# SSD mixer in a hybrid decoder layer: both decay planes of a chunk in one double-buffered tile, one copy of their ends, and convolution tails read from PSUM

## The chip, the core and the metric

The kernel runs on one core of a Trainium2 chip. The metric is the device time of one execution in microseconds; a run's time is that of the whole launch, and the profile's span is from the first to the last instruction. The engines are TensorE (PE; its weight loads are PEld), VectorE (DVE), ScalarE (ACT), GpSimd (POOL), and SyncE (SP), which issues nearly all DMAs.

## The reference

One layer on 2048 tokens of width 1024, in float32. A normalised input goes through one large projection. Its columns feed a sparse attention (an indexer scores keys, the best 256 of each query are kept) and an SSD mixer; both results go through an output projection, and a dense MLP with a squared ReLU follows. Cut to the SSD part:

```python
xbc = conv(xbc)                                  # causal, width 4, depthwise
X = (xs * dt[..., None])                         # 16 chunks of 128 tokens, 8 heads
A_cs = jnp.cumsum(Adt, axis=-1)
Lmat = jnp.exp(segsum(Adt))                      # decays inside a chunk
cb = jnp.einsum("bclhn,bcshn->bhcls", Cc, Bc) * Lmat
y_diag = jnp.einsum("bhcls,bcshp->bclhp", cb, X)
decay_states = jnp.exp(A_cs[..., -1:] - A_cs)
states = jnp.einsum("bclhn,bhcl,bclhp->bchpn", Bc, decay_states, X)
...
y_off = jnp.einsum("bclhn,bchpn,bhcl->bclhp", Cc, states, jnp.exp(A_cs))
y = y_diag + y_off
```

The convolution needs the last three tokens of the tokens before it; these are the tails of the kernel.

## The kernel before, in words

Tokens are worked on in four tiles of 512. A front stage runs `in_proj(t)` for the four tiles. Every product of the large projections is split into high and low parts (`mm3`, L257, L260, L261), which read weights (wr, split by POOL and ACT into wh and wl) and a moving operand u. For each of eight column groups of the convolution (L364 to L374) `raw` receives three old columns from `tails` (L367), the scaled product from PSUM (L329), and then its last three columns are copied to `tails` (L369); three multiply-adds (L374) make `pre`. The results are written to DRAM (s_d).

`ssd(t)` runs 32 pieces in all: 4 tiles x 4 chunks x 2 head groups. A piece has an `enter`, a `carry`, and every second one a `leave`. `enter` loads si (L483) and the cumulative decays cb (L486, the same row in all partitions). VectorE adds a mask, lm = cb + trineg (L487). ScalarE takes four exponentials of lm (L489) and one of cb (L490). VectorE copies the last column of each plane to `ends` (L492, L493). TensorE transposes and multiplies into p_x (L496, L497); VectorE scales it to xd (L500), GpSimd multiplies with ends (L501), VectorE multiplies lm with p_x (L503), and GpSimd cb with si (L504), both in place. `carry` makes p_y from lm, xd, cb and the state st (L514, L515), p_st (L517), updates the state (L518, L519) and adds the skip (L521). `leave` normalises (L530 to L543) and stores to mix_d (L546). lm has one buffer, cb two, si three, xd one.

The back stage runs four windows, each an output projection `out_proj(t)` (p_acc, its eviction L793, the residual sum L802, transposes L807, operands u of the next products L810) and then `mlp(t)` (up products with r, L834, and down products p_dn). Top-k selection (`topk`, L611 to L643: 32 counting passes on ACT with L618 and L619 on DVE behind each, then seven passes L633 to L643 over the scores) and `attention` are woven into front and windows. A pacing function (`weave`) issues their steps at set points with a priority for each kind; a scheduler with a timeline of its own then places the instructions on each engine, so that a change of a wait or of a dependence moves rows elsewhere too. Each engine runs its rows strictly in that order.

Of the kernel before, what the change touches and what calls it, by code (L numbers as in the profile page):

```python
# [16 lines left out]
OP = mybir.AluOpType  # L17
# [4 lines left out]
P = 128  # L22
L = 2048
D = 1024
T = 512
# [16 lines left out]
def hybrid_layer(ctx, tc, x, x_t, w_cols, n_post_mix, n_post_mlp, w_in, w_misc, dt_bias, a_log, d_skip,  # L42
                 w_out, w_up, w_down, rel_bias, c_ident, c_flip, c_stack, c_tri, c_trineg, c_caus, c_bucket, out, dbg=None):
    nc = tc.nc
    V, S, G, PE, SP = nc.vector, nc.scalar, nc.gpsimd, nc.tensor, nc.sync
# [15 lines left out]
    ATT = dict(c2=2, qs=2)  # L61
    FRONT = dict(c4=FC, x24=1, m4=2, m2=3, kc=2, tq=1, mk=1)
    BACK = dict(c4=BC, x8=2, g4=9, m2=2)
    SSD = dict(si=3, cb=2, lm=1, xd=1)
    SIDE = [dict(kc=3, tq=1, mk=1), dict(kc=2, tq=1)]
    BANKS = [dict(tp=3, po=1), dict(tp=3, po=1)]
    where = {}
# [7 lines left out]
    def place(tag):  # L75

        if tag in rings:
            rings[tag].append(rings[tag].pop(0))
            return rings[tag][-1]
        return where[tag]  # L80

    def tl(tag, shape, dt=F32, name=None):
        pool, bufs, slot = place(tag)
        return pool.tile(shape, dt, tag=name if tag in ("s", "ks", "ssm") else slot, name=name or tag, bufs=bufs)

    def phase(name, sizes, smalls=None, side="left"):
        stack = ExitStack()
        pool = stack.enter_context(tc.tile_pool(name=name, bufs=1, side=side, reuse_waits="tile"))
        use(pool, sizes)
        if smalls:  # L90
            use(pool, {smalls: 2})
        return stack

    def once_tile(name, shape, dt=F32):
        return where["ssm"][0].tile(shape, dt, name=name, bufs=1)
# [6 lines left out]
    def pt(tag, name=None):  # L102
        pool, bufs, slot = place(tag)
        return pool.tile([P, 512], F32, tag=slot, name=name or tag, bufs=bufs)
# [15 lines left out]

    scan = phase("scan", SSD, "ssm", "right")
    front = phase("front", FRONT, "s")
# [67 lines left out]
    tails = once_tile("tails", [P, 8, 3])  # L190
# [74 lines left out]
    def proj(ap, u, w=None, how='00'):  # L265

        m = ap.shape[-1]
        w = w or load_w(ap, [P, KT, m], how)
        p = pt("mm", "p_mm")
        for k in range(KT):  # L270
            hi, lo = w[k // 4]
            mm3(p[0:m], hi[:, k % 4, :], lo[:, k % 4, :], u[k][:, 0, :], u[k][:, 1, :], k == 0, k == KT - 1)
        return p
# [13 lines left out]
    def row_spread(rs, tag="mm"):  # L287
        p = pt(tag, "p_rs")
        for b in range(NB):
            PE.matmul(p[:, b * P:(b + 1) * P], rs[:, b:b + 1].broadcast_to([P, P]), ident, start=True, stop=True)  # L290
        rsb = tl("rsb", [P, T])
        V.tensor_copy(rsb, p)
        return rsb
# [26 lines left out]
    def in_proj(t):  # L320
# [5 lines left out]
        else:  # L326
            rsb = row_spread(state["rs", t], TB)
# [4 lines left out]
        p = proj(w_misc, u, w, how=HI_)  # L332
        if t == 0:
            row_scale(0)
            rsb = row_spread(state["rs", 0], "acc")
# [5 lines left out]
        p = pt(TB, "p_tr")  # L341
# [22 lines left out]
        for m in range(8):  # L364
            p = proj(w_in[m], u, how=HI_)
            raw = tl("m2", [P, T + 4], name="raw")
            V.tensor_copy(raw[:, 0:3], tails[:, m, :])  # L367
            scaled(raw[:, 3:T + 3], p)
            V.tensor_copy(tails[:, m, :], raw[:, T:T + 3])  # L369
            acc = pre[:, m, :]  # L370
            tap_w = lambda j: cols[:, 16 + j * 8 + m:17 + j * 8 + m]
            S.activation(acc, raw[:, 3:T + 3], AF.Identity, scale=tap_w(3), bias=cols[:, 48 + m:49 + m])
            for j in range(3):
                V.scalar_tensor_tensor(acc, raw[:, j:T + j], tap_w(j), acc, op0=OP.mult, op1=OP.add)  # L374
            if m == 1:
                p = pt(TB, "p_tr")
                for b in range(NB):
                    PE.transpose(p[0:DH, b * P:(b + 1) * P], ki[:, b, :], ident)
                kf = tl("m2", [DH, T], name="kf")
                S.activation(kf, p[0:DH], AF.Identity, scale=cols[0:DH, 60:61], bias=cols[0:DH, 61:62])  # L380
                hs = KI[0:DH, t0:t0 + T]
                S.activation(hs, kf, AF.Copy)
                V.tensor_tensor(KI[DH:P, t0:t0 + T], kf, hs.bitcast(F32), op=OP.subtract)
            yield 5.2
# [13 lines left out]
        for m in range(4):  # L398
            p = proj(w_in[8 + m], u, how=HI_)
# [9 lines left out]
        p = proj(w_in[12], u, how=HI_)  # L409
# [8 lines left out]
        p = proj(w_in[13], u, how=HI_)  # L418
# [3 lines left out]
        p = pt(TB, "p_tr")  # L422
# [35 lines left out]
    def ssd(t):  # L458
# [4 lines left out]
        p = pt(bank, "p_cs")  # L463
# [5 lines left out]
        p = pt(bank, "p_cs")  # L469
# [9 lines left out]
        def enter(c, g):  # L479

            hs = slice(4 * g, 4 * g + 4)
            si = tl("si", [P, 6, P], name="si")
            SP.dma_start(si, s_d[t, g, :, :, c * P:(c + 1) * P])  # L483
            cb = tl("cb", [P, 4, P], name="cb")
            lm = tl("lm", [P, 4, P], name="lm")
            SP.dma_start(cb, cs_d[c:c + 1, hs].partition_broadcast(P))  # L486
            V.tensor_tensor(lm, cb, cn["trineg"].unsqueeze(1).broadcast_to([P, 4, P]), op=OP.add)  # L487
            for h in range(4):
                S.activation(lm[:, h], lm[:, h], AF.Exp, bias=ncs[:, c, 4 * g + h:4 * g + h + 1])  # L489
            S.activation(cb, cb, AF.Exp)  # L490
            ends = tl("ssm", [P, 2, 4], name="ends")
            V.tensor_copy(ends[:, 0], cb[:, :, P - 1])  # L492
            V.tensor_copy(ends[:, 1], lm[:, :, P - 1])  # L493
            px = pt(bank, "p_x")
            for m in range(3):
                PE.transpose(px[:, m * P:(m + 1) * P], si[:, m], ident)  # L496
            PE.matmul(px[:, 384:512], si[:, 2], si[:, 3], start=True, stop=True)  # L497
            xd = tl("xd", [P, 640], name="xd")
            x0, x1 = xd[:, 0:256], xd[:, 256:512]
            V.tensor_tensor(x3(x0), x3(px[:, 0:256]), bc(dts[:, c, hs], DH), op=OP.mult)  # L500
            G.tensor_tensor(x3(x1), x3(x0), bc(ends[:, 1], DH), op=OP.mult)  # L501
            S.activation(xd[:, 512:640], px[:, 256:384], AF.Copy)
            V.tensor_tensor(lm, lm, px[:, 384:512].unsqueeze(1).broadcast_to([P, 4, P]), op=OP.mult)  # L503
            G.tensor_tensor(cb, cb, si[:, 3].unsqueeze(1).broadcast_to([P, 4, P]), op=OP.mult)  # L504
            return c, g, si, cb, lm, xd, ends
# [42 lines left out]
        parts = [(c, g) for c in range(NB) for g in range(2)]  # L548
        sis = []
        now = enter(*parts[0])  # L550
        yield
        for i in range(len(parts)):
# [21 lines left out]
    def topk(i0, g):  # L574
# [4 lines left out]
        for i in range(i0, i0 + g):  # L579
# [6 lines left out]
            for j0 in range(0, ni, 512):  # L586
                w = min(512, ni - j0)
                for h in range(HI):
                    p = pt("tp", "p_ix")
# [11 lines left out]
                G.memset(sc[:, ni:n], MASKED)  # L601

        cnt = tl("ks", [P, 4], name="cnt")[:, 0:g]

        keep = tl("ks", [P, 4], I32, name="keep")[:, 0:g]
        cnd = tl("ks", [P, 4], I32, name="cnd")[:, 0:g]

# [379 lines left out]
    if NF > 4:  # L987
        tasks.append(ctask(range(4, NF), *PF))
    weave(chain(*(in_proj(t) for t in range(NT))), tasks)
    front.close()  # L990
    state["win"] = "1"
# [97 lines left out]
```

## Time and profile before

| what | value |
|---|---|
| runs | 2932.82 us median of 3 (2929.6 to 2933.56) |
| the profiled execution, its own time | 2928.61 us |
| its span, mean granted TensorE clock | 2926.8 us, 0.977 |
| PE, PEld busy | 2754.8 us (94%), 2240.5 us (77%) |
| DVE, ACT, POOL busy | 1668.1 (57%), 1483.0 (51%), 1775.7 us (61%) |
| DMA | 383.46 MB, mean 131 GB/s |

How to read it: busy time is the time in which an engine has an instruction in work. In the chain of waits every step is followed back to what released it. In the groups of instructions a row is one line, engine and operation, with its number, its busy time and the mean of one, and behind the bar the idle time just before them and what ended it. An arrow `<-` in a wait points to the operation that ended it. `p_` names are PSUM tiles.

### The profile page before, as it was taken

To read this page: it belongs to the slowest core of one execution; us is meant where nothing else is said; L and a number is where in the kernel's file an instruction comes from. 1 tells how busy PE (TensorE), PEld (TensorE's weight loads), DVE (VectorE), ACT (ScalarE), POOL (GpSimd) and SP (SyncE) were. 2 spreads that over 40 slices of the span, in tenths; PEclk is the share of its full clock that TensorE was granted. 3 is DMA by queue.
4 is the path that set the end of the run, shared out by engine and by line. 5 is a ranking of instruction groups with operands and counts; after the bars stand their busy time and mean duration, and the time that the engine had idled before them with its cause. 6 is when DMAs were issued, how large, how long until landed. Compare 5 with 4: busy or idle time off the path is not lost.

```text
span 2926.8 us, 41172 instructions
## 1 busy us (share of the span) xinstructions
PE 2754.8 (94%) x13558; PEld 2240.5 (77%) x13558; DVE 1668.1 (57%) x4106; ACT 1483.0 (51%) x2550; POOL 1775.7 (61%) x1721
## 2 busy tenths in 40 slices
PE   7988989888889999999899999999999999999998
PEld 5766767666668887888688878878888888778886
DVE  6579688878575656657765565666444342511113
ACT  2475577665746586767683847644332332311101
POOL 4666556667656656564457575644564656578775
PEclk9999999989989999999999999999999999999999
DMA  4754754634733333355233222553232225522222
GB/s 131 233 181 142 228 158 132 214 107 166 243 120 116 111 110 97 101 163 191 97 98 103 92 94 81 164 185 102 87 96 80 93 78 177 204 94 97 95 94 87
DMA packets 286741, 383.46 MB, mean 131 GB/s; under 512 B 26520, under 2 KB 151360, under 8 KB 286528
## 3 DMA queue, kind: packets, MB, share of 16 engines
q1 hardware_dynamic: 286528, 380.84, 40.1%
q8 instruction: 107, 1.75, 0.2%
q14 instruction: 106, 0.87, 0.1%
HBM read 316.44 MB, written 64.30 MB: 130 GB/s over the span
## 4 chain that ended last, share of the span: by engine, by line
PE 68%; DVE 13%; ACT 5%; DMA 5%; POOL 4%; issue 4%; SPq 1%; POOLq 0%; DVEq 0%; ACTq 0%
PE p_mm L261 9%; PE p_mm L257 9%; PE p_mm L260 9%; PE p_dn L261 7%; PE p_dn L260 7%; PE p_dn L257 7%; PE p_o L726 4%; PE p_s L684 4%; PE p_pt L718 3%; ACT junk_k L611 3%; POOL wl L232 2%; PE p_ix L591 2%; PE p_acc L257 1%; PE p_acc L260 1%; PE p_acc L261 1%
## 5 line engine op out<-in xcount | busy, mean ns | idle before, releaser
L232 POOL TENSOR_TENSOR wl<-wr,wh 128x512 fp32r<-128x512 f32 (+1 forms) x740 | 994.9, 1345 | 177.6 <-ACT wh L229 112.6
L231 POOL TENSOR_SCALAR wh<-wr 128x512 fp32r<-128x512 f32 x674 | 448.7, 666 | 727.6 <-PE p_mm L260 339.2
L257 PE MATMUL p_mm<-u,wh 128*128 128x512 f32 (+1 forms) x1696 | 680.4, 402 | 38.2 <-ACT u L311 15.4
L261 PE MATMUL p_mm<-u,wl 128*128 128x512 f32 (+1 forms) x1696 | 679.8, 402 | 13.6 <-POOL wl L232 13.5
L260 PE MATMUL p_mm<-u,wh 128*128 128x512 f32 (+1 forms) x1696 | 670.1, 396 | 0.5 <-POOL u L309 0.3
L611 ACT ACTIVATE junk_k<-sc,cnd 128x512 int8<-128x512 f32 (+10 forms) x434 | 576.4, 1328 | 161.7 <-DVE cnd L619 131.5
L260 PE MATMUL p_dn<-wl,g 128*128 128x512 f32 x1008 | 401.8, 399 | 3.5 <-POOL wl L232 3.5
L257 PEld LDWEIGHTS p_mm<-u,wh 128*128 128x128 f32 (+1 forms) x1696 | 321.3, 189 | 108.6 <-POOL wh L231 19.6
L261 PE MATMUL p_dn<-wh,g 128*128 128x512 f32 x1008 | 399.1, 396 | 2.7 <-POOL g L837 2.7
L261 PEld LDWEIGHTS p_mm<-u,wl 128*128 128x128 f32 (+1 forms) x1696 | 320.2, 189 | 88.4 <-POOL wl L232 22.0
L260 PEld LDWEIGHTS p_mm<-u,wh 128*128 128x128 f32 (+1 forms) x1696 | 320.6, 189 | 69.5 <-DVE u L312 2.1
L257 PE MATMUL p_dn<-wh,g 128*128 128x512 f32 x1008 | 328.7, 399 | 1.3 <-POOL wh L231 0.6
L835 ACT ACTIVATE r<-r 128x512 f32<-128x512 f32 x128 | 80.4, 629 | 434.6 <-DVE r L834 434.1
L689 DVE CUSTOM_DVE_ANT_0 pp<-p_s,mk 128x512 f32<-128x512 f32 (+3 forms) x320 | 192.7, 606 | 135.5 <-PE p_s L684 132.0
L720 ACT ACTIVATE ppt<-p_pt 128x512 fp32r<-128x512 f32 (+1 forms) x288 | 155.7, 567 | 209.4 <-PE p_pt L718 172.6
L721 DVE TENSOR_TENSOR ppt<-p_pt,ppt 128x512 fp32r<-128x512 f32 (+1 forms) x288 | 183.0, 654 | 120.8 <-ACT ppt L720 117.9
L260 PEld LDWEIGHTS p_dn<-wl,g 128*128 128x128 f32 x1008 | 189.9, 188 | 46.5 <-POOL wl L232 5.8
L261 PEld LDWEIGHTS p_dn<-wh,g 128*128 128x128 f32 x1008 | 190.0, 188 | 43.2 <-POOL g L837 3.1
L257 PEld LDWEIGHTS p_dn<-wh,g 128*128 128x128 f32 x1008 | 185.8, 189 | 41.9 <-POOL wh L231 2.9
L726 PE MATMUL p_o<-ppt,VV 128*128 128x256 f32 x1088 | 211.8, 295 | 1.1 <-ACT ppt L720 0.7
L618 DVE TENSOR_SCALAR keep<-cnt 128x1 int32<-128x1 f32 (+1 forms) x341 | 69.7, 204 | 234.9 <-ACT junk_k L611 233.5
L837 POOL TENSOR_TENSOR g<-r,g 128x512 fp32r<-128x512 f32 x128 | 170.1, 1330 | 54.4 <-ACT g L836 53.2
(252 smaller groups left out, 4209.6 us busy)
## 6 DMA issues: line engine op xcount, KB each, us to landing
wr<-w_up SPq DMA_DIRECT2D x256, 256.0 KB, 2.6
wr<-w_down SPq DMA_DIRECT2D x256, 256.0 KB, 2.6
wr<-w_in SPq DMA_DIRECT2D x160, 256.0 KB, 2.9
tq<-toep_d SPq DMA_DIRECT2D x128, 128.0 KB, 2.5
qs<-q_d SPq DMA_DIRECT2D x256, 64.0 KB, 2.4
wr<-w_out SPq DMA_DIRECT2D x64, 256.0 KB, 4.0
mix<-mix_d SPq DMA_DIRECT2D x32, 512.0 KB, 8.5
q_d<-qp SPq DMA_DIRECT2D x24, 512.0 KB, 3.8
```

Source lines behind the costliest of these rows:

```text
L231: G.tensor_scalar(dst_hi, src_f, 1.0, 0.0, op0=OP.mult, op1=OP.add)
L232: G.tensor_tensor(dst_lo, src_f, dst_hi.bitcast(F32), op=OP.subtract)
L257: m = PE.matmul(o, ah, bh, start=first, stop=False)
L260: PE.matmul(o, ah, bl, start=False, stop=False)
L261: state["mm3"] = PE.matmul(o, al, bh, start=False, stop=last).ins.name
L611: S.activation(junk_k[:, 0:n], scs[j], AF.Sign, bias=bias(j), accum_out=cnt[:, j:j + 1])
L684: PE.matmul(p[:, 0:w], qs[:, var, hh, :], K1[:, g, j0:j0 + w], start=var == 0, stop=var == 1)
L689: V.tensor_tensor_reduce(out=pp[:, j0:j0 + w], in0=p[:, 0:w], in1=mk[:, j0:j0 + w], scale=1.0, scalar=-3e38, op0=OP.add, op1=OP.max, accum ...
L720: S.activation(pg[:, 0, 0:w], p[:, 0:w], AF.Copy)
L721: V.tensor_tensor(pg[:, 1, 0:w], p[:, 0:w], pg[:, 0, 0:w].bitcast(F32), op=OP.subtract)
L726: PE.matmul(po[:, c0:c0 + 256], VV[:, kk, g, :], pg[:, part, j * 256:(j + 1) * 256], start=kk == 0 and part == 0, stop=kk == nb - 1 and pa ...
L837: G.tensor_tensor(gt[:, 1, :], r, gt[:, 0, :].bitcast(F32), op=OP.subtract)
```

## The change

The two planes of a piece, cb and lm, become the halves of one tile with two buffers, so lm has two buffers where it had one. Their last columns are copied to `ends` by one instruction on both halves, in place of two. The tails of the convolution are computed from the product in PSUM and the row scale, in place of a copy from raw. Nothing else changes; a blank line goes.

```diff
-    SSD = dict(si=3, cb=2, lm=1, xd=1)
+    SSD = dict(si=3, cb=2, xd=1)
...
             V.tensor_copy(raw[:, 0:3], tails[:, m, :])
             scaled(raw[:, 3:T + 3], p)
-            V.tensor_copy(tails[:, m, :], raw[:, T:T + 3])
+            V.tensor_tensor(tails[:, m, :], p[:, T - 3:T], rsb[:, T - 3:T], op=OP.mult)
...
-            cb = tl("cb", [P, 4, P], name="cb")
-            lm = tl("lm", [P, 4, P], name="lm")
+            both = tl("cb", [P, 2, 4, P], name="cb")
+            cb, lm = both[:, 0], both[:, 1]
             SP.dma_start(cb, cs_d[c:c + 1, hs].partition_broadcast(P))
             V.tensor_tensor(lm, cb, cn["trineg"].unsqueeze(1).broadcast_to([P, 4, P]), op=OP.add)
             for h in range(4):
                 S.activation(lm[:, h], lm[:, h], AF.Exp, bias=ncs[:, c, 4 * g + h:4 * g + h + 1])
             S.activation(cb, cb, AF.Exp)
             ends = tl("ssm", [P, 2, 4], name="ends")
-            V.tensor_copy(ends[:, 0], cb[:, :, P - 1])
-            V.tensor_copy(ends[:, 1], lm[:, :, P - 1])
+            V.tensor_copy(ends, both[:, :, :, P - 1])
```

Both planes are called cb in the rows of the changed kernel, since that is the tile's name. Its lines behind the copy of ends are numbered one less than before, and those from the top-k's counting on two less (L611 is L609, L802 is L800, L834 is L832).

The order of instructions moves in many places. ScalarE at the first two SSD pieces, before (L489 the exponentials of lm, L490 that of cb, L611 a counting pass of the top-k, L699 an exponential of the attention):

```order
44 L489 ACTIVATE lm<-lm,adt 128x128 x4
45 L490 ACTIVATE cb<-cb 128x512
46 L611 ACTIVATE junk_k,cnt<-sc,cnd 128x512
47 L311 ACTIVATE u<-xr,cols 128x512 x2
48 L699 ACTIVATE pp,den<-pp,nm 128x128
49 L305 ACTIVATE xr<-xr,cols 128x512
50 L611 ACTIVATE junk_k,cnt<-sc,cnd 128x512
51 L308 ACTIVATE u<-xr 128x512
52 L391 ACTIVATE qp<-qf 128x512
53 L489 ACTIVATE lm<-lm,adt 128x128 x4
54 L490 ACTIVATE cb<-cb 128x512
```

The same place in the changed kernel:

```order
44 L489 ACTIVATE cb<-cb,adt 128x128 x4
45 L490 ACTIVATE cb<-cb 128x512
46 L489 ACTIVATE cb<-cb,adt 128x128 x4
47 L490 ACTIVATE cb<-cb 128x512
48 L609 ACTIVATE junk_k,cnt<-sc,cnd 128x512
49 L311 ACTIVATE u<-xr,cols 128x512 x2
50 L697 ACTIVATE pp,den<-pp,nm 128x128
```

The second piece's exponentials have moved up directly behind the first's; the rows that lay between now follow both.

VectorE at the end of the first output projection, before (mkk, sc and junk_k of 1152 columns are the seven passes that finish the top-k of block 8; o is the eviction of p_acc; L540 and L543 belong to an SSD piece's `leave`):

```order
1468 L636 TENSOR_SCALAR mkk,cnt<-sc,thr 128x1152
1469 L638 TENSOR_SCALAR junk_k<-sc,thr 128x1152
1470 L540 SCALAR_TENSOR_TENSOR si<-si,cols,p_ms 128x128 x2
1471 L637 TENSOR_SCALAR cnt<-cnt 128x1
1472 L639 TENSOR_SCALAR mkk<-sc,thr 128x1152
1473 L543 TENSOR_TENSOR si<-si 128x256
1474 L641 SCALAR_TENSOR_TENSOR sc<-junk_k,cnt 128x1152
1475 L642 SCALAR_TENSOR_TENSOR sc<-sc,junk_k 128x1152
1476 L793 TENSOR_TENSOR o<-p_acc,wt 128x512 x2
1477 L540 SCALAR_TENSOR_TENSOR si<-si,cols,p_ms 128x128 x2
1478 L793 TENSOR_TENSOR o<-p_acc,wt 128x512
1479 L643 SCALAR_TENSOR_TENSOR mkk<-sc,mkk 128x1152
```

In the changed kernel the evictions are at rows 1396 to 1409, the residual sums (xh) follow, and no pass of block 8 stands among them:

```order
1435 L800 SCALAR_TENSOR_TENSOR xh<-o,rs_8814,xh 128x256 x3
1436 L224 SCALAR_TENSOR_TENSOR p_ms<-p_ms,rs_y 128x2
1437 L800 SCALAR_TENSOR_TENSOR xh<-o,rs_8814,xh 128x256 x4
1438 L616 TENSOR_SCALAR keep<-cnt 128x1
1439 L520 SCALAR_TENSOR_TENSOR si<-si,dsk,p_y 128x128 x2
1440 L800 SCALAR_TENSOR_TENSOR xh<-o,rs_8814,xh 128x256 x6
1441 L225 SCALAR_TENSOR_TENSOR rs_s<-p_ms,rs_y 128x2
1442 L518 TENSOR_TENSOR st<-st,p_st 128x256
1443 L800 SCALAR_TENSOR_TENSOR xh<-o,rs_8814,xh 128x256 x3
```

The seven passes have moved behind the operands of the first up products; they now stand in front of the first r (L832):

```order
1496 L634 TENSOR_SCALAR mkk,cnt<-sc,thr 128x1152
1497 L636 TENSOR_SCALAR junk_k<-sc,thr 128x1152
1498 L595 SCALAR_TENSOR_TENSOR sc<-p_ix,wsc,sc 128x512
1499 L210 TENSOR_SCALAR p_ms<-p_ms 128x2
1500 L635 TENSOR_SCALAR cnt<-cnt 128x1
1501 L637 TENSOR_SCALAR mkk<-sc,thr 128x1152
1502 L292 COPY rsb<-p_rs 128x512
1503 L213 TENSOR_SCALAR rs_y<-p_ms 128x2
1504 L595 SCALAR_TENSOR_TENSOR sc<-p_ix,wsc,sc 128x512
1505 L639 SCALAR_TENSOR_TENSOR sc<-junk_k,cnt 128x1152
1506 L832 SCALAR_TENSOR_TENSOR r<-p_mm,rsb 128x512
```

## Rows read from the trace of the kernel before

**Rows 1.** The page: busy time of each engine; the chain's shares by engine.

```profile
PE 2754.8 (94%) x13558; PEld 2240.5 (77%) x13558; DVE 1668.1 (57%) x4106; ACT 1483.0 (51%) x2550; POOL 1775.7 (61%) x1721
...
PE 68%; DVE 13%; ACT 5%; DMA 5%; POOL 4%; issue 4%; SPq 1%; POOLq 0%; DVEq 0%; ACTq 0%
```

**Rows 2.** Windows: stretch, its length, busy us of each engine, clock, DMA.

```profile
core 0: us, PE busy (x) PEld busy (x) DVE busy (x) ACT busy (x) POOL busy (x), PEclk, DMA share, GB/s
500.00:600.00 100.00, 82.93 (x386) 63.38 (x385) 73.93 (x158) 71.90 (x131) 68.28 (x65) 0.90 0.62 202
820.00:840.00 20.00, 9.98 (x54) 7.87 (x52) 19.65 (x38) 5.37 (x16) 11.70 (x9) 0.74 0.42 135
840.00:860.00 20.00, 17.83 (x91) 14.03 (x91) 16.49 (x48) 12.16 (x26) 7.41 (x8) 0.83 0.33 126
900.00:1000.00 100.00, 98.86 (x498) 82.00 (x496) 65.08 (x200) 68.31 (x115) 62.05 (x60) 1.00 0.35 112
2000.00:2200.00 200.00, 200.00 (x1064) 169.38 (x1064) 87.54 (x220) 69.25 (x108) 116.86 (x118) 1.00 0.29 92
```

**Rows 3.** Waits of PE, 0 to 860 us: total, times, longest.

```profile
PE p_x L496 <- DMA si<-s_d: 11.6, 7, 5.3
...
PE p_y L514 <- DVE lm L503: 7.9, 5, 3.3
...
PE p_y L514 <- DVE ends L492: 6.2, 2, 3.3
...
PE p_mm L257 <- DVE raw L329: 2.3, 2, 1.8
```

**Rows 4.** Waits of DVE, 100 to 880 us.

```profile
DVE lm L487 <- PE p_y L515: 17.0, 6, 9.3
...
DVE lm L487 <- PE p_y L514: 1.8, 2, 1.0
```

**Rows 5.** Groups of instructions on DVE, 100 to 900 us.

```profile
L493 DVE COPY ends<-lm 128x4 f32<-128x4 f32 x32 | 11.4, 357 | 4.2 <-ACT lm L489 4.1
...
L492 DVE COPY ends<-cb 128x4 f32<-128x4 f32 x32 | 8.3, 259 | 1.4 <-ACT cb L490 1.4
...
L369 DVE COPY tails<-raw 128x3 f32<-128x3 f32 x24 | 7.3, 310 | 0.1
```

**Rows 6.** Timeline at 763 to 771 us: start, length, instruction, idle before it.

```profile
763.59 0.76 PE L257 MATMUL p_acc<-wh,mix 128*128 128x512 f32 x1 [5.39 <-DMA mix<-mix_d]
...
771.04 0.69 DVE L487 TENSOR_TENSOR lm<-cb,trineg 128x512 f32<-128x512 f32 x1 [9.25 <-PE p_y L515]
```

**Rows 7.** Timeline of PE, 829 to 835 us.

```profile
829.60 0.87 PE L496 MATMUL p_x<-ident,si 128*128 128x128 f32 x3 [5.34 <-DMA si<-s_d]
...
834.16 0.70 PE L514 MATMUL p_y<-lm,xd 128*64 128x128 f32 x4 [3.26 <-DVE lm L503]
```

**Rows 8.** Timeline of DVE, 816 to 832 us: three of the seven passes.

```profile
816.56 1.41 DVE L633 TENSOR_SCALAR_CACHE_REDUCE mkk<-sc,thr 128x1152 bf16<-128x1152 f32 x1
...
824.05 2.60 DVE L641 TENSOR_TENSOR_SCAN sc<-junk_k,cnt 128x1152 f32<-128x1152 int8 x1
...
830.51 1.57 DVE L643 SCALAR_TENSOR_TENSOR mkk<-sc,mkk 128x1152 bf16<-128x1152 f32 x1
```

**Rows 9.** Timeline of ACT and DVE at the first SSD piece.

```profile
160.09 0.61 ACT L490 ACTIVATE cb<-cb 128x512 f32<-128x512 f32 x1
...
160.42 0.69 DVE L503 TENSOR_TENSOR lm<-lm,p_x 128x512 f32<-128x512 f32 x1
161.03 0.16 DVE L492 COPY ends<-cb 128x4 f32<-128x4 f32 x1
```

**Rows 10.** Line 210 on DVE: ns min/median/max; p_ms is in PSUM, var in SBUF.

```profile
L210 DVE TENSOR_SCALAR p_ms<-p_ms x16: 150/155/168, 189.4 to 877.7; 128x2 f32<-128x2 f32 x16
...
L210 DVE TENSOR_SCALAR rs_x<-var x4: 155/158/162, 39.0 to 612.2; 128x4 f32<-128x4 f32 x4
```

**Rows 11.** Timeline of DVE, 852 to 866 us.

```profile
852.79 1.63 DVE L810 SCALAR_TENSOR_TENSOR u<-p_tr,cols,u 128x512 fp32r<-128x512 f32 x2 [0.34 <-ACT u L809]
...
864.89 1.29 DVE L834 SCALAR_TENSOR_TENSOR r<-p_mm,rsb 128x512 f32<-128x512 f32 x2
```

## The prediction

> **What bounds the kernel now.** I read the page's first part and its chain of waits first, then a table of windows, then who waited for whom, and last the timeline at three places. The page says TensorE is busy 94% of the span and holds 68% of the chain that ended last; VectorE holds 13% of it [rows 1]. The windows say where the rest is lost. From 900 us on TensorE is 99 to 100% busy at full clock, while between 500 and 600 us it is busy 82.93 of 100 us, at a mean granted clock of 0.90 [rows 2]. So the code of the change, which runs between 160 and 880 us, lies in the part of the span where TensorE still waits, and after that only TensorE's own work counts. An edit there is worth what TensorE stops waiting. Three waits of TensorE belong to the SSD pieces: the first products (p_x) for the load of si, 11.6 us in 7; the output products (p_y) for the decays lm, 7.9 us in 5; p_y for the decays' ends, 6.2 us in 2 [rows 3]. That is 25.7 us, under 0.9% of the span, and is the most that an edit of the SSD alone can win in waits.
>
> **The change part by part.** All sums are against the profiled execution, 2928.61 us; the median of the runs, 2932.82, stands 4.2 above it.
>
> *One copy of ends instead of two.* The two copies cost VectorE 11.4 and 8.3 us for 32 pieces, 19.7 us, or 0.62 us a piece [rows 5]. One of them goes; the one left moves 8 elements a partition where each moved 4, and between once and twice the old price I take once, because at such sizes 128x2 and 128x4 cost the same [rows 10]. VectorE is freed of 9.8 us. It is not the bound, so what reaches the end lies between 0 and 9.8; I take its share of the chain, 13%: **-1.3 us**. The rest is hidden under TensorE's products, and would come out only where those are missing.
>
> *Two buffers for lm.* Before, VectorE's masked sum (L487) could not start on a piece until the p_y of the piece before had read lm; it waited 17.0 us in 6 for the last of them and 1.8 us in 2 for an earlier one [rows 4], with everything behind it in VectorE's queue. The longest of these is 9.25 us, ended at 771.04; but TensorE itself stood until 763.59 for the load of mix and then had main products ahead of p_y [rows 6], so that one only passes on another's delay and I price it at nothing. Its cover is the output projection's operand load; were that load earlier, the p_y would be too. What TensorE can win is its own waits for lm and ends, 7.9 + 6.2 us, less the 3.26 us at 834.16 that I count further down: 10.8 us. The order on ScalarE shows that the second piece's exponentials now stand directly behind the first's, where eight rows lay between, so the decays are really made a piece ahead. Not every wait has the buffer as its cause (the first piece waits too), so I take half: **-5 us**, ends 0 and -10.8.
>
> *The merged copy waits for both exponentials.* ScalarE does the four exponentials of lm and then the one of cb. Before, the product lm times p_x (L503) could follow the copy of lm's ends at once: it started at 160.42, while cb's exponential ran from 160.09 for 0.61 us [rows 9]. Now the one copy needs cb too, and L503, which overwrites lm, stands behind it; p_y stands behind L503. Queued behind the waiting copy on VectorE are also the maxima of the attention, for which TensorE waits elsewhere. The price is at most the 0.61 us of that exponential in each of 32 pieces, 19.5 us, and nothing where it was done anyway. I take it for the 7 pieces where TensorE was found waiting for lm or ends [rows 3]: **+4.3 us**. GpSimd's product with the ends (L501) waits as long, but only p_st needs it, which stands behind p_y.
>
> A rule speaks against this edit. The Trainium skill (Perfetto Trace Analysis, section Optimizing Scalar/DVE Operations) says that where the vector engine is not saturated but causes bubbles elsewhere, breaking instructions up may let work finish sooner; VectorE's 57% here is such a case, and by the rule the merge should lose. It is the second rival below.
>
> *The order at the end of the first output projection.* This is a side effect, and the largest term. The scheduler places instructions by priority as units come free, so the edits move rows far away from them. Before, the seven passes that finish block 8's top-k (L633 to L643, 1152 elements) stood on VectorE ahead of the last steps of out_proj: they begin at 816.56 and the last one of 1.57 us ends at 832.08 [rows 8]. Meanwhile TensorE waited 5.34 us for si, whose load waits for the store of an older piece that VectorE had to finish behind such passes, then 3.26 us for lm [rows 7]. TensorE lost 12.2 us between 820 and 860, and was granted 0.74 and 0.83 of its clock, so about 17 us of this stretch ran at the lower level of 1.2 GHz [rows 2]. In the changed order the whole tail stands behind L800 (the old L802) and behind all the operands of the first up products. I take the wait for si and half of that for lm: **-7 us**. The ends are 0, and -20.8 us, which is all 12.2 us and half of the 17 us at the lower clock. Late next is the piece itself: p_x, the scaling on VectorE, L503 and p_y follow each other with little other work on TensorE, so some idle time stays.
>
> *Tails from PSUM.* The 32 small copies become 32 products of the same size that read the bank directly; they no longer wait for raw. A 128x2 operation on PSUM has a median of 155 ns and a 128x4 one on SBUF 158 [rows 10], so nothing changes: 32 x 0.003 us. The bank is held one small operation longer, 0.31 us with what it waits [rows 5], and TensorE waited for such a bank twice, 2.3 us [rows 3]; at most +0.6 us, and I take **0**. The Trainium skill (same page and section) puts the access at about 60 ns for SBUF and 125 ns for PSUM, which would add 32 x 65 ns, an estimate of 2.1 us on VectorE. No row here shows that difference, and either value is below what can be measured.
>
> Sum: -1.3 - 5 + 4.3 - 7 = -9.0 us, 2919.6 us for a profiled execution. Runs stand 4.2 us higher: **2924 us**.
>
> **The rivals.** *No change.* The tail of block 8's top-k has not gone: it now stands in front of the first r (L834, now L832), which empties the banks of the up products. Before, 12 us lay between the last operands (852.79) and the first r (864.89) with the banks as cover [rows 11]. Three of the seven passes, the first, the scan and the last, take 1.41 + 2.60 + 1.57 = 5.58 us [rows 8]; with four more at the first one's price it is 11.2 us. If TensorE fills its banks before that, it stops for up to those 11.2 us and the 7 us come back. With the other terms near zero, as VectorE's work is mostly hidden, the time is 2928 to 2938, about 2932. For it: p_y's waits are few. Against: in the rows of the window from 900 us TensorE loses almost nothing, so the later stretch has room. That the change doesn't do what it says (one buffer's use after another as before) would come out here too; the order speaks against it.
>
> *Slower.* The merged copy decides. Where ScalarE is late, each p_y stands behind cb's exponential: 32 x 0.61 = 19.5 us lost, 9.8 us saved on VectorE, and nothing else won gives 2932.8 + 9.7 = about 2942. The place is every piece in which L503 used to start ahead of the copy from cb, as at 160.42 against 161.03 [rows 9]. It decides once more than about half of the 32 pieces reach p_x on TensorE with the decays unfinished. Against it: only 7 waits were found, and the decays are now begun earlier.
>
> **How the numbers follow.** About 0.2% (6 us) is what a measurement of this kernel can tell from no change, so faster means below 2927 and slower above 2938.7. The forecast, whose own range is 2910 to 2927, gets 0.50: its largest terms rest on visible waits, but they are side effects of a changed order, and other waits between 100 and 900 us will be redrawn by the same scheduler in ways that no row tells. No change gets 0.31, slower 0.19. The range 2906 to 2941 takes in the forecast, no change and the near end of slower. It leaves out the far ends of the terms.
>
> **What would show it.** Right: TensorE busier than 9.98 of 20 us and at a higher clock where the first output projection ends; no wait of L487 for p_y; p_y's waits for lm and ends below 14.1 us together; one copy of about 0.3 us mean for 32 pieces; the top-k passes after L800. Wrong: waits of p_y for the copy of ends that have grown to over 10 us; TensorE waiting for r after the first up products; or TensorE's busy time between 100 and 900 us unchanged.

## The result and the profile after

The changed kernel takes **2970.8 us** (median of 4 runs, 2969.1 to 2976.6), the kernel before took 2933.2 beside it (4 runs, 2929.6 to 2937.3): a ratio of 1.0136, 95% interval 1.0121 to 1.0151. It is slower by 1.4%; the prediction said 2924 us, and its range ended at 2941. The profiled execution took 2969.14 us, with a span of 2967.3.

The page of the changed kernel, busy time and chain, against [rows 1]:

```profile
PE 2774.4 (93%) x13558; PEld 2254.4 (76%) x13558; DVE 1668.5 (56%) x4074; ACT 1479.9 (50%) x2550; POOL 1780.5 (60%) x1721
...
PE 65%; DVE 13%; DMA 7%; ACT 6%; issue 4%; POOL 3%; SPq 1%; POOLq 0%; DVEq 0%; ACTq 0%
```

TensorE runs the same 13558 products, with a smaller share of a longer span. VectorE has 32 instructions fewer and is no less busy. The windows of the changed kernel, those of [rows 2] (columns as there) and one for 800 to 900 us, where the kernel before had TensorE busy 87.26 us at a clock of 0.91:

```profile
500.00:600.00 100.00, 83.88 (x378) 63.92 (x377) 69.58 (x151) 63.50 (x119) 68.44 (x69) 0.91 0.62 203
820.00:840.00 20.00, 15.53 (x80) 11.72 (x78) 11.51 (x40) 15.84 (x34) 10.14 (x11) 0.94 0.39 124
840.00:860.00 20.00, 13.43 (x66) 10.79 (x67) 17.35 (x63) 10.43 (x22) 6.28 (x8) 0.50 0.26 88
900.00:1000.00 100.00, 96.91 (x485) 80.24 (x483) 57.25 (x195) 70.91 (x121) 64.76 (x64) 1.00 0.36 114
2000.00:2200.00 200.00, 195.46 (x1047) 164.41 (x1046) 99.49 (x256) 74.90 (x124) 97.39 (x98) 0.98 0.29 94
...
800.00:900.00 100.00, 78.71 (x390) 61.09 (x390) 68.37 (x200) 65.97 (x130) 44.30 (x46) 0.85 0.37 121
```

Where the forecast looked, it came true: between 820 and 840 us TensorE is busy 15.53 us at a clock of 0.94, where it was 9.98 at 0.74. The next 20 us lose it again: 13.43 for 17.83, the whole stretch at the lower level of 1.2 GHz (a granted clock of 0.50, behind a wait of 4.0 us for si at 838). The loss between 2000 and 2200 us is none: the kernel before has the same one 40 us sooner, in its window

```profile
1960.00:2160.00 200.00, 196.38 (x1062) 166.07 (x1060) 101.97 (x268) 79.51 (x132) 98.33 (x99) 0.98 0.29 96
```

and the changed kernel, which runs late by then, has it in the window from 2000 us on. Windows at equal times compare different work once a kernel lags; hence the count of products below.

Who waited for whom in the changed kernel; first TensorE over the whole span, against [rows 3] (the kernel before has none of those waits behind 860 us), then VectorE between 100 and 900 us, against [rows 4]; then VectorE's groups, against [rows 5]:

```profile
PE p_y L513 <- DVE cb L502: 14.8, 11, 3.4
...
PE p_y L513 <- DVE ends L492: 6.6, 1, 6.6
...
PE p_x L495 <- DMA si<-s_d: 4.5, 2, 4.0
```

```profile
DVE cb L487 <- DMA cb<-cs_d: 16.5, 14, 3.1
DVE ends L492 <- ACT cb L490: 10.6, 13, 2.3
```

```profile
L492 DVE COPY ends<-cb 128x8 f32<-128x8 f32 x32 | 8.5, 266 | 10.7 <-ACT cb L490 10.6
L369 DVE TENSOR_TENSOR tails<-p_mm,rsb 128x3 f32<-128x3 f32 x24 | 3.4, 146 | 0.0
```

L487 no longer waits for p_y; it waits for the load of cs_d in its place, 16.5 us in 14 where it was 4.9 in 2. The one copy waits 10.6 us for cb's exponential. A tail takes 146 ns in the mean where it took 310. TensorE's waits of p_y are 21.4 us in 12 (14.8 + 6.6), where they were 14.1 in 7. That is 7.3 us of the 38 that the medians differ by (40.5 by the two spans), so most of the loss lies elsewhere.

To find it I counted the main products of TensorE (p_mm, p_acc and p_dn, 8928 in each kernel) and compared when the n-th starts in the two traces. The lag of the changed kernel is 10.2 us at product 2112 (795 us in the kernel before), 23.4 at 2304 (880 us), 31.1 at 2688 (994 us) and 40.5 at the last. So it comes in steps, the largest at the end of the first output projection. There the timeline of VectorE in the changed kernel shows the tail of block 8's top-k (the seven passes and the short instructions that go with them), which stood at 816 to 832 us before [rows 8]:

```profile
875.41 0.68 DVE L502 TENSOR_TENSOR cb<-cb,p_x 128x512 f32<-128x512 f32 x1
...
884.61 1.40 DVE L631 TENSOR_SCALAR_CACHE_REDUCE mkk<-sc,thr 128x1152 bf16<-128x1152 f32 x1
...
889.49 0.74 DVE L595 SCALAR_TENSOR_TENSOR sc<-p_ix,wsc,sc 128x512 f32<-128x512 f32 x1
...
891.67 0.73 DVE L595 SCALAR_TENSOR_TENSOR sc<-p_ix,wsc,sc 128x512 f32<-128x512 f32 x1
892.33 2.60 DVE L639 TENSOR_TENSOR_SCAN sc<-junk_k,cnt 128x1152 f32<-128x1152 int8 x1
894.85 0.66 DVE L832 SCALAR_TENSOR_TENSOR r<-p_mm,rsb 128x512 f32<-128x512 f32 x1
895.43 0.15 DVE L217 TENSOR_TENSOR p_ms<-p_ms,rs_y 128x2 f32<-128x2 f32 x1
...
900.54 1.82 DVE L641 SCALAR_TENSOR_TENSOR mkk<-sc,mkk 128x1152 bf16<-128x1152 f32 x1
```

and the timeline of TensorE, what it waits for meanwhile (in brackets: idle time before, and who ended it):

```profile
890.28 0.73 PE L590 MATMUL p_ix<-KI,qi 128*128 128x512 f32 x2 [2.25 <-DVE sc L595]
892.46 1.22 PE L590 MATMUL p_ix<-KI,qi 128*128 128x512 f32 x2 [1.44 <-DVE sc L595]
895.66 0.76 PE L257 MATMUL p_mm<-u,wh 128*128 128x512 f32 x1 [1.98 <-DVE p_ms L217]
```

The last row starts 0.15 us after r has emptied a bank of the up products (894.85 + 0.66), and 0.08 us after the p_ms step that the row names (895.43 + 0.15). Both stood behind the scan on VectorE. The two waits ahead of it are for score sums of the indexer (L595), which stood between the passes. The product with p_x that p_y needs (L502) stood ahead of the tail here, and p_y did not wait.

### The profile page after: what moved, and what is told of

Read it like the earlier page. It is cut to its first block, busy times and chain, and to the rows that moved or that the text cites. A ratio compares the mean times of both kernels' runs of the same rounds, so it can differ in the third digit from the quotient of the medians.

```text
span 2967.3 us, 41168 instructions
## 1 busy us (share of the span) xinstructions
PE 2774.4 (93%) x13558; PEld 2254.4 (76%) x13558; DVE 1668.5 (56%) x4074; ACT 1479.9 (50%) x2550; POOL 1780.5 (60%) x1721
## 4 chain that ended last, share of the span: by engine, by line
PE 65%; DVE 13%; DMA 7%; ACT 6%; issue 4%; POOL 3%; SPq 1%; POOLq 0%; DVEq 0%; ACTq 0%
PE p_mm L261 9%; PE p_mm L257 9%; PE p_mm L260 9%; PE p_dn L260 7%; PE p_dn L261 7%; PE p_dn L257 7%; ACT junk_k L609 4%; PE p_s L682 4%; PE p_o L724 4%; PE p_pt L716 3%; POOL wl L232 2%; DVE pre L374 1%; DMA cb<-cs_d 1%; PE p_ix L590 1%; PE p_acc L257 1%
## 5 line engine op out<-in xcount | busy, mean ns | idle before, releaser
L231 POOL TENSOR_SCALAR wh<-wr 128x512 fp32r<-128x512 f32 x674 | 456.6, 678 | 754.1 <-PE p_mm L260 345.6
L257 PE MATMUL p_mm<-u,wh 128*128 128x512 f32 (+1 forms) x1696 | 683.6, 404 | 33.5 <-ACT u L311 15.8
L609 ACT ACTIVATE junk_k<-sc,cnd 128x512 int8<-128x512 f32 (+10 forms) x434 | 576.6, 1329 | 175.4 <-DVE cnd L617 135.1
L616 DVE TENSOR_SCALAR keep<-cnt 128x1 int32<-128x1 f32 (+1 forms) x341 | 80.1, 235 | 254.2 <-ACT junk_k L609 253.2
L697 ACT ACTIVATE pp<-pp,nm 128x128 f32<-128x128 f32 (+15 forms) x128 | 153.2, 1197 | 117.7 <-DVE nm L694 105.1
```

The source lines that it names most:

```text
L231: G.tensor_scalar(dst_hi, src_f, 1.0, 0.0, op0=OP.mult, op1=OP.add)
L257: m = PE.matmul(o, ah, bh, start=first, stop=False)
L609: S.activation(junk_k[:, 0:n], scs[j], AF.Sign, bias=bias(j), accum_out=cnt[:, j:j + 1])
L697: S.activation(pp, pp, AF.Exp, bias=nm, accum_out=den[:, h:h + 1])
```

## Experiments: parts of the change, and an edit that costs nothing

Three theories stood at the start. A: any edit makes the scheduler draw the order anew, and the time goes with the order. B: the merged copy holds p_y back. C: the tails hold PSUM banks longer. Four kernels, each the kernel before with one edit. `e1_tails` has the tails alone:

```diff
-            V.tensor_copy(tails[:, m, :], raw[:, T:T + 3])
+            V.tensor_tensor(tails[:, m, :], p[:, T - 3:T], rsb[:, T - 3:T], op=OP.mult)
```

> The kernel before with only the convolution tails computed from PSUM. Theory A (the order: the changed kernel loses because the scheduler, given any edit, places rows elsewhere, above all the seven top-k passes in front of the first r): this edit redraws the order too, so its time is off from before by up to 20 to 40 us either way, though its own operations cost nothing. Theory B (the merged copy holds p_y back): 2933 us within 6, since nothing in the SSD changed. Theory C (the banks are held longer): about 2970, all of the loss.

`e2_ssd` has the SSD edits alone, that is the whole diff without the line of the tails:

> The changed kernel with the tails copied from raw as before, so both SSD edits alone. Theory A: off from before by up to 20 to 40 us, not the same figure as the changed kernel. Theory B: about 2970, the whole loss. Theory C: about 2933.

`e3_lm2` keeps two tiles and two copies and gives lm its second buffer:

```diff
-    SSD = dict(si=3, cb=2, lm=1, xd=1)
+    SSD = dict(si=3, cb=2, lm=2, xd=1)
```

> The kernel before with two buffers for lm, as two tiles and with two copies of the ends, tails as before. Theory B (the merged copy): faster than before by the 5 to 11 us that the second buffer frees, about 2925. Theory A: anything within some 30 us of before, by where the order falls. A third reading (working two pieces deep itself is what costs): about 2960 to 2970.

`n2_swap` only exchanges two statements that write different columns of raw:

```diff
-            V.tensor_copy(raw[:, 0:3], tails[:, m, :])
             scaled(raw[:, 3:T + 3], p)
+            V.tensor_copy(raw[:, 0:3], tails[:, m, :])
```

> The kernel before with two independent statements of the convolution in the other order (the scaled product into raw, then the three old columns). The same instructions with the same waits; only what the scheduler makes of them differs. Theory A: the time moves clear of noise, by 10 us or more in either direction. Theories B and C: 2933 within 6 us.

Measured beside a kernel before at 2935.8 us (7 runs):

| kernel | median us | ratio, 95% interval |
|---|---|---|
| e1_tails | 2951.5 | 1.0056, 1.0036 to 1.0075 |
| e2_ssd | 2968.2 | 1.0122, 1.0103 to 1.0141 |
| e3_lm2 | 2976.6 | 1.0141, 1.0121 to 1.0161 |
| n2_swap | 2974.3 | 1.0142, 1.0123 to 1.0161 |

An exchange of two independent statements costs as much as the whole change. A second buffer, which takes nothing from the kernel, costs as much too. Neither has the merged copy or the tails. B and C can't be the cause of these; A can. Not all of A's figures came: `e3_lm2` lies 41 us above the kernel before, where A gave some 30, and `e2_ssd` has the changed kernel's time, which A did not expect and which, taken alone, fits B. The traces show the order redrawn by the exchange: `n2_swap` has the same instructions as the kernel before, and on TensorE 6537 of the 13558 places in the sequence hold another kind of instruction. But it is not yet shown that the changed kernel's own loss is the order, since its operations differ too.

## Experiments: the operations in the other kernel's order

The next kernels fix the order. A table gives each engine call the place that it had in another kernel, and each engine's instructions are chained in that order by edges that order only and wait for nothing. The scheduler's priorities and one edge between the main products, which served the same end, go:

```diff
+                r = _ranks[_at[0]]
+                _at[0] += 1
+                now = tc.tile_snap_priority()
+                with tc.high_priority(now + 200000 - r):
+                    ins = f(*a, **k)
+                _placed.append((r, ins.ins))
...
     weave(window(3), [])
+    last = {}
+    for _, ins in sorted(_placed, key=lambda e: e[0]):
+        if ins.engine in last:
+            tc.add_manual_dep(ins, last[ins.engine], NOSYNC, reason="the order")
+        last[ins.engine] = ins.name
```

All engine calls go through one helper, so rows of these kernels carry its line (L277 or L266), and in those with the changed kernel's operations lm has cb's name, as both lie in one tile. `b_in_after_order` has lm's second buffer too, in a tile of its own.

> The changed kernel's operations, all of them, with each engine's instructions put in the order of the kernel before: the order is the same on PE, ScalarE, GpSimd and SyncE, and on VectorE but for the 32 copies that the change removes (the merged copy stands where the copy of lm's ends stood) and the conv tails' operand. Theory A (the loss is the order that the scheduler made of the change, the operations cost about nothing): 2925 to 2940 us, within 0.3% of the kernel before. Theory B (the merged copy's wait for both exponentials, or the shared tile, costs the time): 2960 to 2975. Theory C (tails from PSUM hold the banks longer): about 2950, as the tails alone gave 2951.5.

> The operations of the kernel before (two copies of ends, tails from raw, two tiles), lm with two buffers, with each engine's instructions put in the order of the changed kernel (the two copies side by side where the merged one stood). Theory A: about 2970, as the changed kernel, plus at most 10 us of 32 more small copies on VectorE. Theories B and C: 2935 to 2950, since the merged wait and the tails from PSUM are gone.

Then two kernels with the changed kernel's operations and its order in a part of the program only:

> The changed kernel's operations; order of the kernel before up to its 2112th main product (795 us there), then the changed kernel's order up to its 2400th (931 us there, 907 in the kernel before), then the order of the kernel before for what is left. Theory A with a place (the later top-k tail of block 8 and what is queued behind it cost their time here): by the lag of the changed kernel's products, +10.2 us at 2112 and +24.1 at 2400, this stretch alone gives about +14: 2945 to 2952. If the lag there is only shifted, and would come back later: 2930 to 2938. If it is the order everywhere a little: about +3.

> The changed kernel's operations; order of the kernel before up to its 2400th main product, then the changed kernel's order to the end. Theory A with places: lag +24.1 at 2400 and +40.5 at the end of the two traces, so +12 to +18: 2946 to 2953. If the stretch before product 2400 holds the whole loss: 2930 to 2938.

Beside a kernel before at 2934.7 us (15 runs):

| kernel | median us | ratio, 95% interval |
|---|---|---|
| a_in_before_order | 2934.9 | 1.0002, 0.9991 to 1.0014 |
| b_in_after_order | 2977.2 | 1.0143, 1.0126 to 1.0159 |
| order_2112_2400 | 2952.1 | 1.0065, 1.0051 to 1.0079 |
| order_from_2400 | 2956.0 | 1.0072, 1.0059 to 1.0085 |

This settles the main question. In the trace of `a_in_before_order` TensorE, ScalarE and GpSimd run the kinds of instruction of the kernel before in its very sequence, and VectorE too but for the merged copies and the tails. The changed operations in the old order take the old time; the old operations in the new order take the new time. **In either order the operations are worth nothing that can be measured, and the order is worth the whole loss.** One thing is not taken apart: no kernel has the new order with a single buffer for lm, and the orders that the scheduler drew for two buffers (the changed kernel's, `e2_ssd`'s, `e3_lm2`'s) are all slow, so what the second buffer might give in a better one is open. The page and the waits of `a_in_before_order`:

```profile
PE 2766.8 (94%) x13558; PEld 2249.9 (77%) x13558; DVE 1660.1 (57%) x4074; ACT 1483.4 (51%) x2550; POOL 1779.3 (61%) x1721
```

```profile
PE p_y L277 <- DVE cb L277: 15.1, 8, 3.8
...
PE p_x L277 <- DMA si<-s_d: 9.1, 7, 5.4
```

VectorE is 8.0 us less busy than before [rows 1], and the time is the same. p_y waits 15.1 us where it waited 14.1 [rows 3].

The partial orders put part of the loss into the stretch between products 2112 and 2400, and more of it behind. The first is at the upper end of what was expected, the second 3 us above it. The second holds something of its own: in that trace 7 us come within 32 products of the seam, where the changed kernel loses 1.2. So the two are not to be added up.

## Experiments: one tail moved

In the stretch from 2112 to 2400 the most visible move was block 8's tail. Four kernels have the changed kernel's operations and differ in where that tail stands.

> The changed kernel's operations in the order of the kernel before, but for the last eight counting passes of block 8's top-k and the tail behind them (42 instructions): these stand, by the count of main products issued, where the changed kernel has them, so that the scan follows product 2282 and not 2208. Theory 'the late tail' (block 8's top-k ends in front of the first r of the up products, and PE waits for VectorE there): +8 to +14 us, 2941 to 2949, with the lag coming between products 2208 and 2304. Rival 'the rest of the stretch' (other operations that were redrawn between products 2112 and 2400 cost the time, VectorE has room for the tail): within 3 us of the kernel before.

> The counterpart: the kernel whose order between main products 2112 and 2400 is the changed kernel's, with those 42 instructions put back to where the kernel before has them (scan behind product 2208). Theory 'the late tail': most of the loss of that stretch (2952.1 against 2934.7, 17.4 us) goes and +3 to +8 stays: 2938 to 2943. Rival 'the rest of the stretch': 2949 to 2955, as without putting them back.

Measured beside a kernel before at 2937.5 us (9 runs): tail_late 2948.5, ratio 1.0037 (1.0024 to 1.0051); tail_back 2950.4, ratio 1.0046 (1.0032 to 1.0060). So tail_late confirms the late tail, and tail_back contradicts it: putting the tail back did not return the time, or less of it than the two intervals can tell (order_2112_2400 had 1.0051 to 1.0079). The lag of main products says how, worked out as above against the trace of `a_in_before_order`, in us:

| product | starts at | changed kernel | order_2112_2400 | tail_late | tail_back | tail_spread | tail_spread_8 |
|---|---|---|---|---|---|---|---|
| 2112 | 798 | 6.3 | -1.4 | -3.2 | 3.1 | 1.0 | 0.4 |
| 2208 | 856 | 10.0 | 4.6 | -5.9 | 15.8 | -2.9 | -1.9 |
| 2272 | 873 | 10.9 | 5.4 | -4.0 | 17.0 | -2.7 | 0.2 |
| 2304 | 885 | 19.1 | 14.0 | 10.9 | 18.1 | -2.7 | 2.6 |
| 2400 | 912 | 19.8 | 14.4 | 10.9 | 18.5 | 1.0 | 6.3 |
| last | 2923 | 34.2 | 15.7 | 15.5 | 15.6 | 1.6 | 9.4 |

How far to trust such a lag: all kernels of the table but the changed one have the reference's order up to product 2112 and from 2400 on. At 2112 they still lie between -3.2 and 3.1 us, and behind 2400 they drift by -2.9 to 4.6. Between 2112 and 2400 the lag is steadier: two other traces with the reference's order there, those of the kernel before and of order_from_2400, keep theirs to within 0.8 us.

In tail_late, 42 instructions moved and nothing else: 2.7 us are won in front of product 2208 and 14.9 lost between 2272 and 2304, in one place. In tail_back most of the loss lies in front of 2208 (12.7 us). Between 800 and 910 us TensorE waits there 5.3 us for si and 6.3 for the product with p_x, where the reference has 6.7 and 3.3, and also 2.8 for evictions (o) and 3.4 for residual sums (xh), where the reference has none and 0.3. VectorE's work between products 2112 and 2208 is about the same in both, some 57 and 56 us; what differs is the order on the engines. Which rows of it cost the time was not tried. The timeline of VectorE in tail_late, around the long operations:

```profile
871.42 1.40 DVE L266 TENSOR_SCALAR_CACHE_REDUCE mkk<-sc,thr 128x1152 bf16<-128x1152 f32 x1
...
873.14 0.42 DVE L266 TENSOR_TENSOR xd<-p_x,dts 128x256 f32<-128x256 f32 x1
...
876.67 1.75 DVE L266 TENSOR_SCALAR mkk<-sc,thr 128x1152 bf16<-128x1152 f32 x1
878.45 3.50 DVE L266 TENSOR_TENSOR_SCAN sc<-junk_k,cnt 128x1152 f32<-128x1152 int8 x1
881.88 0.66 DVE L266 TENSOR_TENSOR cb<-cb,p_x 128x512 f32<-128x512 f32 x1
```

of GpSimd:

```profile
873.63 0.61 POOL L266 TENSOR_TENSOR xd<-xd,ends 128x256 f32<-128x256 f32 x1 [4.92 <-DVE xd L266]
874.22 0.62 POOL L266 TENSOR_SCALAR wh<-wr 128x512 fp32r<-128x512 f32 x1
```

and of TensorE:

```profile
874.89 1.22 PE L266 MATMUL p_mm<-u,wh 128*128 128x512 f32 x2 [3.56 <-POOL wh L266]
882.59 0.70 PE L266 MATMUL p_y<-cb,xd 128*64 128x128 f32 x4 [6.48 <-DVE cb L266]
```

Two short instructions stand among the passes. The scaling of xd, 0.42 us, comes behind the first one; GpSimd waits 4.92 us for it, with the split of the next weights (wh) behind that in its queue, and TensorE stops for 3.56 us. The product with p_x, 0.66 us, stands behind the scan; p_y needs it, and TensorE stops for 6.48 us. In the reference TensorE has neither wait. The two waits are 10.0 of the 14.9 us. What is left fits the clock: between 880 and 900 us TensorE is granted 0.71, against 1.00 in the reference, and 0.29 of 20 us is an estimate of 5.8 us, part of it while TensorE stood. The two windows (columns as in [rows 2]), tail_late first:

```profile
880.00:900.00 20.00, 17.41 (x75) 14.43 (x76) 11.94 (x24) 4.50 (x8) 10.63 (x10) 0.71 0.20 68
880.00:900.00 20.00, 20.00 (x96) 16.66 (x95) 12.19 (x28) 7.42 (x15) 15.96 (x17) 1.00 0.39 121
```

So what the tail costs here hangs on two short instructions that stood behind parts of it. Two last kernels tested that, and whether it gives a kernel faster than both:

> The changed kernel's operations in the order of the kernel before, but with block 8's tail (16 instructions, from the threshold's clean-up to the write of the mask) taken out of the stretch in front of main product 2208 and set between products 2286 and 2353, one long operation every 4 to 10 products, behind the SSD piece's product with p_x there and not in front of it. Theory 'what stands behind it in VectorE's queue' (the tail costs where an eviction, an SSD piece or an si buffer's release waits behind it, not by its own 15 us): the 5.4 us wait for si and part of the 3.3 us wait for cb in front of product 2208 go, and nothing comes at 2286 to 2353: 2 to 8 us faster than the kernel before, 2927 to 2933. Rival 'VectorE is full wherever it goes': 2935 to 2948.

> As tail_spread, and the last eight counting passes at the changed kernel's later places as in tail_late. Theory 'what stands behind it': the 15 us that tail_late lost between products 2272 and 2304 don't come, its 2.7 us gain in front of 2208 stays: 2927 to 2933. Rival 'VectorE is full': as tail_late, 2945 to 2952.

Beside a kernel before at 2935.5 us (22 runs): tail_spread 2938.5, ratio 1.0007 (0.9997 to 1.0018); tail_spread_8 2942.5, ratio 1.0023 (1.0014 to 1.0033). With the tail gone from in front of product 2208, TensorE's waits there shrink, from 5.43 and 3.27 us in `a_in_before_order` (first two rows) to 3.61 and 1.55 in tail_spread (last two):

```profile
833.93 0.88 PE L277 MATMUL p_x<-ident,si 128*128 128x128 f32 x3 [5.43 <-DMA si<-s_d]
838.50 0.70 PE L277 MATMUL p_y<-cb,xd 128*64 128x128 f32 x4 [3.27 <-DVE cb L277]
```

```profile
832.79 0.87 PE L266 MATMUL p_x<-ident,si 128*128 128x128 f32 x3 [3.61 <-DMA si<-s_d]
835.63 0.70 PE L266 MATMUL p_y<-cb,xd 128*64 128x128 f32 x4 [1.55 <-DVE cb L266]
```

3.9 us are won by product 2208 (from 1.0 to -2.9), about what the two waits shrank by, and 3.7 given back between 2304 and 2400, where VectorE, now with the tail, is the busy one. Its window in tail_spread (third column of busy times):

```profile
880.00:900.00 20.00, 18.17 (x78) 13.27 (x76) 19.30 (x35) 6.03 (x12) 13.46 (x11) 1.00 0.29 87
```

So the theory held for the large loss: in tail_spread_8, which differs from tail_late in where the 16 instructions stand, 2.4 us came between 2272 and 2304 in place of 14.9. It failed for the gain. tail_spread came out at 2938.5 where the theory said 2927 to 2933 and the rival, "VectorE is full wherever it goes", 2935 to 2948; tail_spread_8 lies between the two theories' ranges. Neither is faster than the kernel before, and I found no order that is.

What stays open: which moves cost the 6.3 us ahead of product 2112 (by the spread above, 3 to 10) and the 14 us from 2400 on in the changed kernel. That they are moves, and not operations, `a_in_before_order` shows; no single one was tried. Open too is why the old order is the best of those tried.

## Why the prediction was wrong

**The step that failed is "The order at the end of the first output projection"**, and with it how the redrawing of all other places was treated. That step took the tail's old place, priced what TensorE lost there at -7 us, and set the new place at nothing. The mechanism at the old place was right, its size about half: with the tail alone gone from there, 2.7 us were won (tail_late) and 3.9 (tail_spread). In the changed kernel even that did not come, as it lost 3.7 us on the reference between products 2112 and 2208, with other rows redrawn there. The new place cost the changed kernel 8.2 us (between products 2272 and 2304) and 14.9 when the tail moved alone. The rival "No change" had named it (the tail in front of r), with a bound of 11.2 us, and its 8.2 us is within that; r was one of the rows that TensorE waited for, the indexer's score sums were the others. But the rival let it only take back the 7 us, and so foresaw a draw.

That is one place of several. Of the 34.2 us that the changed kernel lags behind the reference, 6.3 came ahead of product 2112 and 14.4 behind 2400 (912 us). So the first paragraph's "after that only TensorE's own work counts", of the time from 900 us on, failed as well (nor did it hold of all that time before, with TensorE busy 36.38 of 40 us from 1960 to 2000): the lag grows by 6.6 us up to product 2688 (999 us) alone, and order_from_2400, in which nothing ahead of product 2400 is redrawn, is 0.7% slower, of which the seam can be at most 7 us of 21. The text says that other waits "will be redrawn by the same scheduler in ways that no row tells", between 100 and 900 us, and gave that no term and no width. That unpriced remark was the result. A neutral edit measures it, at +1.4%; five different edits of this kernel lost 0.6 to 1.4%. The range held no redrawing at all.

The other steps, by the runs in a fixed order:

- *One copy of ends.* Predicted 9.8 us of VectorE and -1.3 of time. In the same order the copies went from 19.7 us [rows 5] to 11.7: 128x8 took 365 ns in the mean where 128x4 took 259 and 357, so 8.0 us were freed. In time: part of a total of 0.02%, interval -0.09 to 0.14. The groups of the copies and of the tails in `a_in_before_order`:

```profile
L277 DVE COPY ends<-cb 128x8 f32<-128x8 f32 x32 | 11.7, 365 | 10.7 <-ACT cb L277 10.6
L277 DVE TENSOR_TENSOR tails<-p_mm,rsb 128x3 f32<-128x3 f32 x32 | 4.7, 148 | 0.0
```

- *Two buffers for lm.* Predicted -5. In the same order L487's waits for p_y, 18.8 us, are gone and nothing has come in their place (5.0 us for the load of cs_d, 4.9 before); in the changed kernel's own order the load's wait rose to 16.5 us. p_y waits 15.1 us in the same order, 14.1 before. So the waits of VectorE that went were not what TensorE waited for.
- *The merged copy's wait.* Predicted +4.3. The copy does wait, 10.6 us in 12 pieces. At the first piece the 0.61 us shows: the timeline of `a_in_before_order` has cb's exponential, the copy and then the product with p_x, where the product started during the exponential before [rows 9]:

```profile
163.42 0.61 ACT L277 ACTIVATE cb<-cb 128x512 f32<-128x512 f32 x1
164.06 0.17 DVE L277 COPY ends<-cb 128x8 f32<-128x8 f32 x1 [1.29 <-ACT cb L277]
164.27 0.69 DVE L277 TENSOR_TENSOR cb<-cb,p_x 128x512 f32<-128x512 f32 x1
```

  Over all pieces TensorE's waits of p_y are 1 us longer (15.1 for 14.1). Both this step and the second buffer are in that figure, predicted together at -0.7; no run parts them. The rival "Slower" had the right sign by the wrong mechanism: its 2942 us rested on this wait. The rule of the Trainium skill that was weighed there (Perfetto Trace Analysis, Optimizing Scalar/DVE Operations: breaking instructions up may finish sooner) is neither borne out nor contradicted by this case, since in one order merged and split take the same time: 1.0002 in the old order, and in the new one 1.0136 merged and 1.0143 split.
- *Tails from PSUM.* Predicted 0 in time, and 0 in the same order. But "nothing changes" was read from medians (they are 160 ns and, in the same order, 149). The means are 389 and 148, so VectorE is freed of 7.7 us (12.4 to 4.7 over all 32). The +0.6% of `e1_tails` is taken to be the order's; the tails alone were not run in the old order. The group before, over the whole span:

```profile
L369 DVE COPY tails<-raw 128x3 f32<-128x3 f32 x32 | 12.4, 389 | 0.3
```

Of the signs that were named, those of the place came out right (TensorE at 820 to 840 us, the passes behind L800, no wait of L487 for p_y, one copy of 0.27 us); p_y's waits (21.4 us in place of less than 14.1, though those for the copy of ends, 6.6, stayed under the 10 that were named), and TensorE waiting for r and the score sums behind the first up products, came out as the signs of being wrong.

## What to carry to other kernels

Where a scheduler draws the order, an edit has two prices: that of its operations, and that of the new order. Exchange two independent statements and time that: if the neutral edit moves the time by more than the sum of the terms, the sum predicts nothing, and the edit is to be measured with the order held fixed. And when a long block that nobody waits for moves, look at what stands behind and between its parts in its engine's queue at the new place: the same tail cost 15 us around two short instructions that TensorE's operands hung on, and under 4 where it stood behind them in pieces.

## What the runs showed that was not expected

That the order of this kernel matters so much: five redrawn orders lay 16 to 41 us above it and none below, though each runs the same products on the same engines. And that moving the tail out of a stretch in which VectorE was busy 19.65 of 20 us [rows 2] won only 3.9 us there: the waits for si and cb became 1.8 and 1.7 us shorter and did not go. I take it that the piece's own chain of load, transposes, scaling and product remained; no run shows that.

And why VectorE's small copies took so unevenly long. In the kernel before, 40 of the 128 copies of ends and tails between SBUF tiles (L367, L369, L492, L493) took over 250 ns, up to 1267. Each of the 40 lay across a running GpSimd instruction and ended 22 to 29 ns behind that one's end. Of the 32 products that read the tails from PSUM, 21 lay across a GpSimd instruction in `a_in_before_order`, and none took over 157 ns. Whether the memory or the kind of operation makes the difference was not tried.
